# Attention scores by head strips with gate tiles between the levels, and the first MLP product by seven products of blocks

## The chip, the cores and the metric

The kernel runs on one core of one Trainium2 chip. The metric is the device time of one execution in microseconds (us); before the change three runs gave 1222.52, 1223.50 and 1223.92, median 1223.5. Engines: PE is TensorE (matrix products into PSUM; PEld its weight loads), DVE is VectorE, ACT is ScalarE, POOL is GpSimd, and SP is SyncE, which here only issues DMAs.

## The reference

One layer of a hybrid backbone for 512 sample tokens and 128 prompt tokens (640 columns in the kernel, `NT`; half of them is `HN` = 320), width 1024, all in float32:

```
h  = rmsnorm(x) * (1 + sc1) + sh1                    # modulated by c or c_ctx (ada_w, 1024 x 6144)
u  = h @ w_in                                        # 1024 x 6432
y  = pooling, Fourier, RWKV-7 (two directions, scan over chunks), GLA (two directions)
GLA: att[t,s] = sum_d q[t,d] k[s,d] decay[t,s,d], 4 heads of 32; o = att @ v + state term
merged = sum_i sigmoid(u_gate[i]) * (y[i] @ w_branch[i])   # 4 branches, 4 x 1024 gate columns of w_in
x  = x + g1 * (merged @ w_out)
h2 = rmsnorm(x) * (1 + sc2) + sh2
x  = x + g2 * (relu(h2 @ mlp_w1)**2 @ mlp_w2)        # 1024 x 4096, 4096 x 1024
y  = rmsnorm(x) * final_g
```

## The kernel before, in words

**Products in two parts.** A large product is made of three: both operands are split into a rounded part (fp32r, `..h`) and a remainder (`..l`), and h*h, h*l and l*h are added in PSUM. A weight tile goes through `load` (L249): `fetch` (L238) issues one DMA on SP into one of three buffers "wr" (128 x 512 floats, 256 KB), and `split` (L244) makes the rounded part on ACT (L246) and the remainder on DVE (L247). `terms` (L363) issues the three products on both halves of the columns, so a tile of 8 blocks of rows is 48 products of 320 columns: this is a column tile of `w_in`, and a gate tile. A branch tile has two blocks, 12 products.

**Order.** The code is traced in program order, and a list scheduler lays down each engine's queue at build time: of what is ready in its model, the earliest traced first. `with hi()` lifts what it traces above that order, `high_priority(offset=...)` shifts it by a number (a negative one lets it fill what others leave), and `tc.issue_after(ins)` lets the instructions traced in it that run on the engine of `ins` stand behind `ins` there. A pool with `bufs=n` gives a tag n buffers; the next tile waits until the oldest is released. At run time each queue is worked off in its order.

**Stages.** (1) Norm, modulation, input projection (`columns` writes 15 tiles to DRAM, `uscr`), pooling and Fourier. (2) RWKV in two pairs of heads (L686): a scan of 8 steps (L915) of small products; `new_x` (L848) copies values into the next state tile on POOL (L854). Gate and branch tiles of branches 0 and 1 and gate tiles of branch 2 (L1218 to L1224), traced later, fill PE meanwhile; gates of branch 2 go to DRAM (`gscr`) and come back for `merged(2, ...)` (L1226). (3) GLA: for each of seven levels (L1056; half sizes p = 64 down to 1) `eq` and `ek` are made on DVE and ACT, `eq` is copied head by head into a tile `eqm` that is zero outside a head's 32 partitions (L1080), and for each of the five token tiles one product of 512 columns (4 heads x 128) gives the scores (L1084), of which a masked copy (L1091 on DVE, for the two first levels L1089 on ACT) goes to `att`. Then states and outputs to L1176. (4) Last branch and output projection (L1252): per `dt` the gate tiles of branch 3, two ahead (L1254), branch 3, the sum of all branches split in two parts (L1263, L1264), two tiles of `w_out`, and products for four token tiles (L1247); `ada_rest` (L319) makes part of the modulation on DVE (L309) from 256 KB tiles. (5) Second half of that projection, residual, norm, transposes into `nh` and `nl` (L1326).

**MLP.** Four groups of 8 column tiles. `hidden` (L1356) makes one column tile for one half of the tokens: 24 products (L1361), then ReLU on ACT, square on DVE, and the split into `fh` and `fl` (L1365 to L1368). Then the second product of the group (L1407) for two halves of the output columns, 5 token tiles each, in five banks; `residual` (L1392) multiplies each sum with g2 and adds it to `xf` in two DVE passes. The last half of the last group has its weights at hand (L1416) and is followed tile by tile by the last norm and the output.

Of the kernel before, what the change touches and what calls it, by code (L numbers as in the profile page):

```python
# [14 lines left out]
ALU = mybir.AluOpType  # L15
# [121 lines left out]
def backbone(ctx, tc, a, y_prompt, y_sample, out_rwkv, out_gla):  # L137
# [100 lines left out]
    def fetch(src):  # L238
        n, c = src.shape[1:]
        raw = wpool.tile([P, 512], F32, name="wr", tag="wr", bufs=3)[:, : n * c].rearrange("p (k c) -> p k c", c=c)  # L240
        nc.sync.dma_start(out=raw, in_=src)
        return raw

# [118 lines left out]

    def terms(pt, wh, wl, k, c0, mh, ml, start, stop):  # L363

        lh, ll = wh[:, k, c0 : c0 + P], wl[:, k, c0 : c0 + P]
        for n, (w, m) in enumerate(((lh, mh), (lh, ml), (ll, mh))):
            for b in range(2):
                PE.matmul(pt[:, b, :HN], lhsT=w, rhs=m[:, b * HN : b * HN + HN],  # L368
                          start=start and n == 0, stop=stop and n == 2)
# [252 lines left out]

    def split_into(y, j, src):
# [62 lines left out]
    for hp in range(2):  # L686
# [161 lines left out]
        def new_x(step):  # L848

            x = upool.tile([P, 4, 2, 2, 64], F32, name="xc", tag="xc", bufs=3)  # L850
            for smp in (True, False)[: 2 if step < 2 else 1]:
                ch = slice(0, 2) if smp else slice(2, 4)
                for O_, par in ((HR[0], 1), (HR[1], 0)):
                    (S.copy if step == 0 else G.tensor_copy)(x[O_, ch, par], pick(VT, step, smp)[O_].unsqueeze(2).broadcast_to([64, 2, 2, 64]))  # L854
# [130 lines left out]

    pb.close()
# [23 lines left out]
    eqm = [gpool.tile([P, 4, NT], F32, name=f"eqm{j}") for j in range(2)]  # L1010
# [45 lines left out]
    for n in range(7):  # L1056
# [18 lines left out]
        else:  # L1075
            ek = kg
        em = eqm[n % 2]
        for h in range(4):
            hr = slice(32 * h, 32 * h + 32)
            S.copy(em[hr, h, :], eq[hr, :])  # L1080
        for i in range(5):
            ts_ = slice(i * P, i * P + P)
            pt = pxt()
            PE.matmul(pt, lhsT=ek[:, ts_], rhs=em[:, :, ts_], start=True, stop=True)  # L1084
            pt = pt.rearrange("p (h t) -> p h t", h=4)
            if p >= 32:
                for s0 in range(0, P, p):
                    rows, cols = slice(s0, s0 + p), slice(s0 ^ p, (s0 ^ p) + p)
                    S.copy(att[rows, :, i, cols], pt[rows, :, cols])  # L1089
            else:  # L1090
                V.copy_predicated(att[:, :, i, :], lm[:, n, :].unsqueeze(1).broadcast_to([P, 4, P]), pt)  # L1091
# [86 lines left out]

    def load_y(n, pool=mgpool):
        y = new_y(pool)  # L1180
        for j in range(2):
            t = zpool.tile([P, NT], F32, name="mg", tag="mg", bufs=2)
            nc.sync.dma_start(out=t, in_=yscr[n][j])
            split_into(y, j, t)
        return y

    def gate(i, dt):
        pt = proj(C_GATE + i * D + dt * P)
        g = zpool.tile([P, NT], F32, name="gate", tag="gate", bufs=3)
        with hi():  # L1190
            S.activation(v2(g), pt, AF.Tanh, scale=0.5)
        return g

    def branch(i, dt, y):
        bh_, bl_ = load(a["t_branch"][i, dt], wpool, "b", 1)
        pt = pm.tile([P, 2, 512], F32, name="pt", tag="pm")
        for k in range(2):
            terms(pt, bh_, bl_, k, 0, y[0][:, k, :], y[1][:, k, :], k == 0, k == 1)
        return pt

    gscr = [dpool.tile([P, NT], F32, name=f"gscr{k}") for k in range(KT)]

    def load_sum(n, dt):
        m = zpool.tile([P, NT], F32, name="mg", tag="mg", bufs=2)
        nc.sync.dma_start(out=m, in_=mscr[n][dt])
        return m

    def gated(g, pt):
        V.scalar_tensor_tensor(v2(g), v2(g), 1.0, pt[:, :, :HN], ALU.add, ALU.mult)

    def merged(i, dt, g, pt):
        with hi():
            gated(g, pt)
            if i > 0:
                V.tensor_tensor(g, load_sum(i - 1, dt), g, ALU.add)
            nc.sync.dma_start(out=mscr[i][dt], in_=g)

    for i, y in ((0, y_a), (1, load_y(0))):  # L1218
        for dt in range(KT):
            merged(i, dt, gate(i, dt), branch(i, dt, y))  # L1220
    for dt in range(KT):
        g = gate(2, dt)
        with hi():
            nc.sync.dma_start(out=gscr[dt], in_=g)  # L1224
    y_r = load_y(2, yrpool)
    for dt in range(KT):  # L1226
        g = zpool.tile([P, NT], F32, name="gate", tag="gate", bufs=3)
        nc.sync.dma_start(out=g, in_=gscr[dt])
        merged(2, dt, g, branch(2, dt, y_r))
# [20 lines left out]
    gates = [gate(3, 0), gate(3, 1)]  # L1250
    accs = [po.tile([P, 512], F32, name="po", tag="po") for _ in range(4)]
    for dt in range(KT + 2):  # L1252
        if dt + 2 < KT:
            gates.append(gate(3, dt + 2))  # L1254
# [28 lines left out]
    nh = h2.tile([P, KT, NT], F32R, name="nh")  # L1283
    nl = h2.tile([P, KT, NT], F32R, name="nl")
    pf1 = ctx.enter_context(tc.tile_pool(name="pf1", bufs=3, space=PSUM, reuse_waits="tile"))
    ops = ExitStack()
# [14 lines left out]
    def projected(i, hf, acc, t):  # L1301
        c = i // 4
        if c not in g1b:
            g1b[c] = h2.tile([P, D], F32, name="g1b", tag="g1b")
# [4 lines left out]
        S.activation(t[:, bs], xf[i][:, bs], AF.Square, accum_out=ss[:, 2 * i + hf : 2 * i + hf + 1])  # L1309

# [14 lines left out]

    def transposed(i, t):  # L1326
        c = i // 4
        sl_ = slice(i * P, i * P + P)
        for k4 in range(2):
# [3 lines left out]
            tm = op.tile([P, 4, P], F32, name="tm", tag="tm", bufs=2)  # L1333
            for k in range(4):
                kk = k4 * 4 + k
                S.activation(tm[:, k], pt[:, k * P : k * P + P], AF.Identity, scale=s2[:, kk, c : c + 1], bias=b2[:, kk, c : c + 1])
            ks = slice(k4 * 4, k4 * 4 + 4)
            S.copy(nh[:, ks, sl_], tm)
            V.tensor_tensor(nl[:, ks, sl_], tm, f32(nh[:, ks, sl_]), ALU.subtract)
# [14 lines left out]
    with tc.tile_pool(name="mlp", bufs=1, reuse_waits="tile") as mp, \  # L1354
            tc.tile_pool(name="pf2", bufs=5, space=PSUM, reuse_waits="tile") as pf2:
        def hidden(w, h, l, b):  # L1356
            pt = pbank()
            bs = slice(b * HN, b * HN + HN)
            for k in range(KT):
                for n, (wk, m) in enumerate(((w[0], nh), (w[0], nl), (w[1], nh))):  # L1360
                    PE.matmul(pt[:, :HN], lhsT=wk[:, k, :], rhs=m[:, k, bs], start=k == 0 and n == 0,  # L1361
                              stop=k == KT - 1 and n == 2)
            with hi():
                rl = mp.tile([P, HN], F32, name="rl", tag="rl", bufs=3)
                S.activation(rl, pt[:, :HN], AF.Relu)  # L1365
                V.tensor_tensor(rl, rl, pt[:, :HN], ALU.mult)  # L1366
                S.copy(h[:, bs], rl)
                V.tensor_tensor(l[:, bs], rl, f32(h[:, bs]), ALU.subtract)  # L1368

        g2b = mp.tile([P, 2, D], F32, name="g2b")  # L1370
        gf = mp.tile([P, D], F32, name="gf")
        NG = 4
        for g in range(NG):
            ws, fh, fl = [], [], []
            order = [(f, b) for f in range(8) for b in range(2)]
            if g == 0:
                order[:4] = [(0, 0), (1, 0), (0, 1), (1, 1)]
            for f, b in order:
                if b == 0:
                    ws.append(load(a["t_w1"][g * 8 + f]))  # L1380
                    fh.append(mp.tile([P, NT], F32R, name="fh", tag="fh", bufs=11))
                    fl.append(mp.tile([P, NT], F32R, name="fl", tag="fl", bufs=11))
                elif f == 0 and g == 0:
# [86 lines left out]
```

## Time and profile before

| | |
|---|---|
| median of three runs | 1223.5 us |
| the profiled execution, its own time | 1224.66 us |
| its span, first to last instruction | 1222.9 us |
| mean granted clock of TensorE | 0.988 |
| instructions | 19633 |
| DMA | 147.41 MB, mean 121 GB/s |

The span is read from the start of the first instruction; the stages meet at about 536 (GLA), 614 (its last level), 650 (last branch), 731, 767 (MLP) and 1213 (last product). Busy time of an engine is the union of its instructions; products are pipelined, so the mean time of one (309 ns) is longer than the step from one to the next (147 ns).

### The profile page before, as it was taken

Reading aid. Unit: us, or ns where it says so; the run is one execution under the profiler, and the core shown is the slowest. Engines: PE = TensorE matmul, PEld = TensorE weight load, DVE = VectorE, ACT = ScalarE, POOL = GpSimd, SP = SyncE. Lnnn points to the kernel's source line nnn. Section 1 sums busy time; section 2 is a strip of 40 time slices with the busy share of each in tenths; the row PEclk is TensorE's granted clock in tenths of the full one; section 3 lists DMA queues with packets and bytes.
Section 4 is the critical chain, followed back from the end, with each engine's and each line's share of the span. In section 5 each row is a group of like instructions: output and inputs, shape, how many; then the busy total and the mean of one; then the engine's idle time right before and its main releaser. Section 6 shows DMA issues by size and latency. Waiting matters only on the chain.

```text
span 1222.9 us, 19633 instructions
## 1 busy us (share of the span) xinstructions
PE 1176.4 (96%) x7556; PEld 1017.1 (83%) x7556; DVE 733.5 (60%) x1458; ACT 506.7 (41%) x1028; POOL 62.3 (5%) x98
## 2 busy tenths in 40 slices
PE   7999999899999999997999989999999999999996
PEld 2778998789778898795588978998899899889985
DVE  4797785675588583447987757543443354245456
ACT  4732225742376522378635325532143123213332
POOL 0000000500114200300000000000000000000000
PEclk9999898999999999999999999999999999999999
DMA  9558661334314343056624560322222222222222
GB/s 357 205 173 251 201 224 57 104 93 119 101 36 122 103 148 95 30 170 212 195 93 141 179 208 18 99 75 69 77 79 85 71 79 78 70 87 69 78 87 86
DMA packets 85971, 147.41 MB, mean 121 GB/s; under 512 B 21693, under 2 KB 26206, under 8 KB 85878
## 3 DMA queue, kind: packets, MB, share of 16 engines
q1 hardware_dynamic: 85878, 146.16, 37.8%
q8 instruction: 59, 0.97, 0.3%
q14 instruction: 34, 0.28, 0.1%
HBM read 123.17 MB, written 22.95 MB: 119 GB/s over the span
## 4 chain that ended last, share of the span: by engine, by line
PE 77%; DVE 8%; DMA 7%; ACT 4%; issue 3%; SPq 0%; POOL 0%; DVEq 0%; ACTq 0%; POOLq 0%
PE pt L368 23%; PE pf L1361 18%; PE pf L1407 16%; PE po L1247 3%; PE pf L1427 2%; PE px L1084 2%; DMA araw<-in_t_ada_dram 2%; PE px L499 2%; DVE acc L309 2%; DVE wl L247 1%; PE px L287 1%; DMA wr<-in_t_in_dram 1%; DMA wr<-in_t_out_dram 1%; DMA wr<-in_t_w_dram 1%; PE px L775 1%
## 5 line engine op out<-in xcount | busy, mean ns | idle before, releaser
L246 ACT CAST wh<-wr 128x512 fp32r<-128x512 f32 x222 | 133.4, 618 | 349.5 <-PE pf L1407 139.1
L247 DVE TENSOR_TENSOR wl<-wr,wh 128x512 fp32r<-128x512 f32 x222 | 152.2, 700 | 206.9 <-ACT wh L246 202.4
L368 PE MATMUL pt<-xl,wh 128*128 128x320 f32 x816 | 200.5, 321 | 0.0
L368 PE MATMUL pt<-xh,wh 128*128 128x320 f32 x816 | 199.7, 321 | 0.0
L368 PE MATMUL pt<-xh,wl 128*128 128x320 f32 x816 | 196.1, 318 | 0.0
L1361 PE MATMUL pf<-nh,wl 128*128 128x320 f32 x512 | 158.1, 309 | 0.0
L1361 PE MATMUL pf<-nl,wh 128*128 128x320 f32 x512 | 158.0, 309 | 0.0
L1361 PE MATMUL pf<-nh,wh 128*128 128x320 f32 x512 | 157.9, 309 | 0.0
L368 PEld LDWEIGHTS pt<-xh,wh 128*128 128x128 f32 x816 | 138.9, 191 | 8.8 <-issue 4.1
L368 PEld LDWEIGHTS pt<-xl,wh 128*128 128x128 f32 x816 | 139.5, 191 | 6.8 <-issue 3.0
L368 PEld LDWEIGHTS pt<-xh,wl 128*128 128x128 f32 x816 | 138.9, 191 | 4.9 <-issue 1.7
L1407 PE MATMUL pf<-wl,fh 128*128 128x512 f32 x280 | 109.0, 389 | 0.0
L1407 PE MATMUL pf<-wh,fh 128*128 128x512 f32 x280 | 109.0, 389 | 0.0
L1407 PE MATMUL pf<-wh,fl 128*128 128x512 f32 x280 | 108.9, 389 | 0.0
L1361 PEld LDWEIGHTS pf<-nl,wh 128*128 128x128 f32 x512 | 96.0, 187 | 0.2
L1361 PEld LDWEIGHTS pf<-nh,wh 128*128 128x128 f32 x512 | 96.0, 188 | 0.1
L1361 PEld LDWEIGHTS pf<-nh,wl 128*128 128x128 f32 x512 | 96.0, 187 | 0.0
L309 DVE SCALAR_TENSOR_TENSOR acc<-araw,sc,acc 128x512 f32<-128x512 f32 x112 | 78.4, 746 | 11.9 <-DMA araw<-in_t_ada_dram 11.9
L1407 PEld LDWEIGHTS pf<-wh,fl 128*128 128x128 f32 x280 | 52.6, 188 | 11.0
L1407 PEld LDWEIGHTS pf<-wh,fh 128*128 128x128 f32 x280 | 52.6, 188 | 10.9
L1407 PEld LDWEIGHTS pf<-wl,fh 128*128 128x128 f32 x280 | 52.6, 188 | 10.7
L1366 DVE TENSOR_TENSOR rl<-rl,pf 128x320 f32<-128x320 f32 x64 | 31.0, 484 | 39.0 <-ACT rl L1365 39.0
(540 smaller groups left out, 1754.2 us busy)
## 6 DMA issues: line engine op xcount, KB each, us to landing
wr<-in_t_w_dram SPq DMA_DIRECT2D x128, 256.0 KB, 3.0
wr<-in_t_in_dram SPq DMA_DIRECT2D x102, 256.0 KB, 3.5
araw<-in_t_ada_dram SPq DMA_DIRECT2D x64, 256.0 KB, 3.5
adaw<-in_t_ada_dram SPq DMA_DIRECT2D x16, 512.0 KB, 9.2
mscr<-gate SPq DMA_DIRECT2D x24, 320.0 KB, 4.3
mg<-mscr SPq DMA_DIRECT2D x24, 320.0 KB, 3.8
uscr<-mg SPq DMA_DIRECT2D x15, 320.0 KB, 2.8
wr<-in_t_branch_dram SPq DMA_DIRECT2D x32, 128.0 KB, 2.1
```

The costliest lines, as they stand in the source:

```text
L246: S.copy(wh, raw)
L247: V.tensor_tensor(wl, raw, f32(wh), ALU.subtract)
L287: PE.matmul(pt[0:8, :], lhsT=c[:, 4 * part : 4 * part + 8, k + j], rhs=w[:, j], start=part == 1 and k + j == 0 and n == 0, stop=part == 0 ...
L309: V.scalar_tensor_tensor(acc[j], raw, w, acc[j], ALU.mult, ALU.add)
L368: PE.matmul(pt[:, b, :HN], lhsT=w, rhs=m[:, b * HN : b * HN + HN], start=start and n == 0, stop=stop and n == 2)
L499: PE.matmul(pt[:, :HN], lhsT=lhsT, rhs=rhs[:, b * HN : b * HN + HN], start=True, stop=True)
L1084: PE.matmul(pt, lhsT=ek[:, ts_], rhs=em[:, :, ts_], start=True, stop=True)
L1247: PE.matmul(acc, lhsT=m[k][:, sl_], rhs=W[k, hf][w][:, 0, :], start=k == 0 and n == 0, stop=k == KT - 1 and n == 2)
L1361: PE.matmul(pt[:, :HN], lhsT=wk[:, k, :], rhs=m[:, k, bs], start=k == 0 and n == 0, stop=k == KT - 1 and n == 2)
L1366: V.tensor_tensor(rl, rl, pt[:, :HN], ALU.mult)
L1407: PE.matmul(acc[i], lhsT=m[k][:, ts_], rhs=w[:, kk, :], start=k == 0 and n == 0, stop=k == 7 and n == 2)
L1427: PE.matmul(acc, lhsT=m[k][:, ts_], rhs=ws[k][w][:, 0, :], start=k == 0 and n == 0, stop=k == 7 and n == 2)
```

## The change

**Scores.** Of each level, the four sample token tiles are now computed per head as strips: 32 partitions of `ek` against the same 32 of `eq`, 128 x 128 scores each, 16 products into four PSUM banks, one per head. Only the prompt's token tile still goes through `eqm` (now 128 columns) into a fifth bank; the pool has four. Copies to `att` stay as many.

**Gates.** The tiles of branches 0 and 1 and the gates of branch 2 are traced before GLA at a priority lowered by 200000. The gate tiles of branch 3 are no longer made in the last stage: tile n - 1 stands on PE behind the prompt's product of level n - 1, and the strips of level n stand behind it. They go to DRAM and come back in the last stage; tiles 6 and 7 follow the levels. Weight tiles of branch 2 get three buffers of their own.

**First MLP product.** `mlp_w1` is laid out as 2 x 2 blocks (`kh`: half of the rows; `fh_`: which of the two column tiles of a pair), 16 pairs. Seven products of 12 give both column tiles for both halves of the tokens (Strassen's scheme in Winograd's form). Four products use sums of weight blocks, read from DRAM tiles `wsum`. For the first group these are made by eight DRAM-to-DRAM DMAs on POOL's queue (four copies, four accumulating), one behind a copy of `new_x` per step of the scan; for the others, DVE adds them during the second product of the group before, with loads on SP and stores on POOL's queue. Five block sums of the normalised input are made on DVE and ACT after the last transposes, while the first three pairs take the products that need none; the transposes write a plain tile `nf`, and `nh`, `nl` keep the first 320 tokens only.

**Residual.** `xf` is stored to DRAM (`xres`) and holds the plain MLP sum (ACT copy in the first group, one DVE pass in the next two); g2 and the stored residual are applied in the last group.

```diff
-        "t_w1": blocks(x["mlp_w1"][0], range(0, FF, P), P),
+        "t_w1": np.ascontiguousarray(blocks(x["mlp_w1"][0], range(0, FF, P), P).reshape(16, 2, P, 2, 512).transpose(3, 1, 0, 2, 4)),
...
+        def begin(n, g):
+            src = w1b[(0, 0, 1, 1)[n], (0, 1, 1, 0)[n], 4 * g : 4 * g + 4]
+            return lambda: nc.gpsimd.dma_start(out=rows(wsum[n][g]), in_=rows(src))
+
+        def add(n, g):
+            src = (w1b[0, 1, 4 * g : 4 * g + 4], w1b[1, 1, 4 * g : 4 * g + 4], wsum[0][g], wsum[2][g])[n]
+            return lambda: nc.gpsimd.dma_start(out=rows(wsum[n][g]), in_=rows(src), accum_op=ALU.add, max_dma_last_dim=8192)
...
+            if step > 0:
+                chore(1, last)
...
+    with tc.high_priority(offset=-200000):
+        for i, y in ((0, y_a), (1, load_y(0))):
+            for dt in range(KT):
+                merged(i, dt, gate(i, dt), branch(i, dt, y))
+        for dt in range(KT):
+            gate_out(0, dt)
...
+        banks = [pxt() for _ in range(4)]
+
+        if n > 0:
+            with tc.issue_after(scored.ins):
+                gate_out(1, n - 1)
+        with hi(), tc.issue_after(newest[0].ins) if n > 0 else ExitStack():
+            for i in range(4):
+                ts_ = slice(i * P, i * P + P)
+                for h in (3, 2, 1, 0):
+                    hr = slice(32 * h, 32 * h + 32)
+                    PE.matmul(banks[h][:, ts_], lhsT=ek[hr, ts_], rhs=eq[hr, ts_], start=True, stop=True)
+
         em = eqm[n % 2]
         for h in range(4):
             hr = slice(32 * h, 32 * h + 32)
-            S.copy(em[hr, h, :], eq[hr, :])
-        for i in range(5):
-            ts_ = slice(i * P, i * P + P)
-            pt = pxt()
-            PE.matmul(pt, lhsT=ek[:, ts_], rhs=em[:, :, ts_], start=True, stop=True)
+            S.copy(em[hr, h, :], eq[hr, NS:])
+        bank = pxt()
+        scored = PE.matmul(bank, lhsT=ek[:, NS:], rhs=em.rearrange("p h t -> p (h t)"), start=True, stop=True)
...
-    gates = [gate(3, 0), gate(3, 1)]
+    gates = [gate_back(1, 0), gate_back(1, 1)]
...
+        put("22", a22)
+        V.tensor_tensor(a22, a22, a21, ALU.subtract)
+        put("22-21", a22)
+        V.tensor_tensor(a21, a11, a21, ALU.subtract)
+        V.scalar_tensor_tensor(a11, a22, -1.0, a11, ALU.mult, ALU.subtract)
+        put("21-22-11", a11)
+        put("11-21", a21)
+        V.scalar_tensor_tensor(a12, a11, -1.0, a12, ALU.mult, ALU.subtract)
+        put("22-21+11-12", a12)
...
+        def product(pt, m, src, first):
+
+            with hi():
+                wh, wl = load(src.unsqueeze(1), mp, "st", 4)
+                wh, wl = wh[:, 0], wl[:, 0]
+            mh_, ml_ = A[m]
+            for k in range(4):
+                ks = slice(k * P, k * P + P)
+                for n, (w, x) in enumerate(((wh, mh_), (wh, ml_), (wl, mh_))):
+                    PE.matmul(pt[:, :HN], lhsT=w[:, ks], rhs=x[:, k, :], start=first and k == 0 and n == 0,
+                              stop=k == 3 and n == 2, skip_group_check=True)
...
+        def pair_steps(j):
...
+            product(ba, "11", b11, True)
+            with hi():
+                S.copy(p1, ba)
+            yield
+            product(bb, "21-22-11", wsum[2][g][q], True)
+            with hi():
+                V.tensor_tensor(u2, p1, bb, ALU.add)
+            yield
+            product(ba, "12", b21, False)
...
+            product(bc, "22-21", wsum[0][g][q], True)
+            product(bb, "11-21", wsum[1][g][q], False)
+            with hi():
+                V.tensor_tensor(u3, p1, bb, ALU.add)
+                c = st()
+                V.tensor_tensor(c, u3, bc, ALU.add)
+                S.activation(c, c, AF.Relu, scale=-1.0)
+                S.activation(c, c, AF.Square)
+                parts_of(c, h1, l1, t1)
+            yield
+            product(bb, "22", wsum[3][g][q], False)
...
+            product(bc, "22-21+11-12", b22, False)
...
+            def weight_sums(g, q):
+
+                b11, b12, b21, b22 = (trp.tile([P, 512], F32, name="tr", tag="tr", bufs=4) for _ in range(4))
+                with tc.issue_after(loaded[0].ins):
+                    for t, (kh, fh_) in ((b11, (0, 0)), (b12, (0, 1)), (b22, (1, 1)), (b21, (1, 0))):
+                        nc.sync.dma_start(out=t, in_=w1b[kh, fh_, 4 * g + q])
+                for n, t, s in ((0, b11, b12), (1, b12, b22), (2, b22, b11), (3, b21, b22)):
+                    V.tensor_tensor(t, t, s, ALU.add)
+                    nc.gpsimd.dma_start(out=wsum[n][g][q], in_=t)
```

## Rows read from the trace of the kernel before

**Rows 1.** The page, busy time (us), share of the span and instructions.
```profile
PE 1176.4 (96%) x7556; PEld 1017.1 (83%) x7556; DVE 733.5 (60%) x1458; ACT 506.7 (41%) x1028; POOL 62.3 (5%) x98
```

**Rows 2.** The chain that ended last: start us, us, what.
```profile
605.58 8.85 PE px L1084 x20
...
742.75 0.87 PE pf L1332 x8
...
756.31 10.90 PE po L1247 x48
...
880.40 56.32 PE pf L1361 x384
```

**Rows 3.** Stages: us, busy us and count per engine, PE clock, DMA share, GB/s.
```profile
300.00:352.00 52.00, 51.42 (x621) 39.66 (x621) 28.00 (x71) 22.18 (x54) 5.45 (x12) 1.00 0.21 62
...
552.00:614.00 62.00, 53.73 (x201) 32.44 (x200) 53.84 (x91) 46.26 (x90) 0.00 (x0) 0.97 0.62 194
614.00:650.00 36.00, 33.61 (x229) 29.48 (x228) 30.01 (x54) 15.26 (x25) 0.00 (x0) 1.00 0.32 101
650.00:731.00 81.00, 77.86 (x440) 68.84 (x440) 52.39 (x81) 29.84 (x51) 0.00 (x0) 0.98 0.57 187
...
826.00:880.00 54.00, 54.00 (x239) 44.68 (x238) 19.54 (x32) 9.74 (x18) 0.00 (x0) 1.00 0.25 78
880.00:936.00 56.00, 56.00 (x383) 55.95 (x382) 27.56 (x53) 21.82 (x46) 0.00 (x0) 1.00 0.25 76
...
1158.00:1185.00 27.00, 27.00 (x121) 22.37 (x120) 11.24 (x18) 9.17 (x16) 0.00 (x0) 1.00 0.35 107
```

**Rows 4.** Stages, products of L368 alone: us, PE and PEld busy us and count.
```profile
552.00:614.00 62.00, 23.47 (x121) 17.92 (x119) 0.97 0.62 194
614.00:650.00 36.00, 20.39 (x114) 17.17 (x114) 1.00 0.32 101
650.00:731.00 81.00, 52.87 (x336) 51.01 (x336) 0.98 0.57 187
```

**Rows 5.** ACT in order of time, the casts of w21 and w27.
```profile
1174.24 0.62 ACT L246 CAST w21h<-wr 128x512 fp32r<-128x512 f32 x1 [1.18 <-DMA wr<-in_t_w_dram]
...
1182.64 0.62 ACT L246 CAST w27h<-wr 128x512 fp32r<-128x512 f32 x1 [0.98 <-DMA wr<-in_t_w_dram]
```

**Rows 6.** Groups by line and shape: count | busy us, mean ns | idle before.
```profile
L247 DVE TENSOR_TENSOR wl<-wr,wh 128x512 fp32r<-128x512 f32 x222 | 152.2, 700 | 206.9 <-ACT wh L246 202.4 <-PE pt L368 3.6 <-issue 0.2
L246 ACT CAST wh<-wr 128x512 fp32r<-128x512 f32 x222 | 133.4, 618 | 349.5 <-PE pf L1407 139.1 <-PE pt L368 113.4 <-PE pf L1361 59.7
...
L1368 DVE TENSOR_TENSOR fl<-rl,fh 128x320 fp32r<-128x320 f32 x64 | 31.5, 492 | 14.2 <-ACT fh L1367 14.2
...
L775 PE MATMUL px<-sl,big 64*128 64x128 f32 x160 | 18.2, 290 | 5.9 <-ACT sl L781 3.4 <-DVE big L757 2.1 <-ACT big L758 0.2
L1091 DVE COPY_PREDICATED att<-lm,px 128x512 f32<-128x512 int32 x25 | 17.2, 735 | 0.4
...
L283 DVE TENSOR_TENSOR adal<-adaw,adah 128x1024 fp32r<-128x1024 f32 x8 | 9.7, 1221 | 2.1 <-ACT adah L282 2.1
```

**Rows 7.** ACT in order of time, the last tokens' modulation.
```profile
775.62 1.19 ACT L1336 ACTIVATE tm<-pf,b,s 128x128 f32<-128x128 f32 x3
```

**Rows 8.** The page, GB/s moved in 40 equal slices.
```profile
GB/s 357 205 173 251 201 224 57 104 93 119 101 36 122 103 148 95 30 170 212 195 93 141 179 208 18 99 75 69 77 79 85 71 79 78 70 87 69 78 87 86
```

**Rows 9.** DMA issues: count, KB each, median us to landing.
```profile
wr<-in_t_w_dram SPq DMA_DIRECT2D x128, 256.0 KB, 3.0
...
gate<-gscr SPq DMA_DIRECT2D x8, 320.0 KB, 4.6
```

**Rows 10.** PE in order of time, half-array products in the scan's preparation.
```profile
231.69 1.25 PE L775 MATMUL px<-sl,big 64*128 64x128 f32 x16 [0.48 <-DVE big L757]
232.87 0.56 PE L368 MATMUL pt<-xh,wl 128*128 128x320 f32 x2
233.27 0.45 PE L368 MATMUL pt<-xh,wh 128*128 128x320 f32 x2
```

More of the change, by code (lines that the diff above doesn't have):

```diff
@@ L1009, in backbone @@
     G.memset(att, 0.0)
-    eqm = [gpool.tile([P, 4, NT], F32, name=f"eqm{j}") for j in range(2)]
+    eqm = [gpool.tile([P, 4, P], F32, name=f"eqm{j}") for j in range(2)]
     for j in range(2):
@@ L1176, in backbone @@
         V.scalar_tensor_tensor(y_out[j], og[j], 0.5, y_out[j], ALU.mult, ALU.mult)
[L1179 to L1224, printed above, removed]
+    for dt in (6, 7):
+        gate_out(1, dt)
     y_r = load_y(2, yrpool)
     for dt in range(KT):
-        g = zpool.tile([P, NT], F32, name="gate", tag="gate", bufs=3)
-        nc.sync.dma_start(out=g, in_=gscr[dt])
-        merged(2, dt, g, branch(2, dt, y_r))
+        merged(2, dt, gate_back(0, dt), branch(2, dt, y_r))
     y_g = new_y()
@@ L1253, in backbone @@
         if dt + 2 < KT:
-            gates.append(gate(3, dt + 2))
+            gates.append(gate_back(1, dt + 2))
         if dt < KT:
@@ L1324, in project, with block_sums, put @@
             projected(i, hf, acc, t)
+    def block_sums(pool):
+        a11, a12, a21, a22 = nf[:, 0:4, t0], nf[:, 4:8, t0], nf[:, 0:4, t1], nf[:, 4:8, t1]
+        r = {}
+        def put(name, s):
+            h, l = (pool.tile([P, 4, HN], F32R, name=f"{n}{name}") for n in ("sh", "sl"))
+            S.copy(h, s)
+            V.tensor_tensor(l, s, f32(h), ALU.subtract)
+            r[name] = (h, l)
+        put("22", a22)
[7 more added lines that the diff above has]
+        put("22-21+11-12", a12)
+        return r
+    t0, t1 = slice(0, HN), slice(HN, NT)
     def transposed(i, t):
@@ L1372, in backbone @@
         NG = 4
         for g in range(NG):
-            ws, fh, fl = [], [], []
-            order = [(f, b) for f in range(8) for b in range(2)]
+            fh, fl = [], []
+            before_ = None
             if g == 0:
[L1377 to L1383, printed above, removed]
-                    with hi():
-                        transposed(4, before)
-                    ops.close()
-                hidden(ws[f], fh[f], fl[f], b)
@@ L1388, in backbone @@
-            if g == 0:
+                now = first_pairs()
+                next(now)
+                with hi():
+                    transposed(4, before)
+                    ops.close()
+                    A.update(block_sums(spool.enter_context(tc.tile_pool(name="spool", bufs=1, reuse_waits="tile"))))
+                nfs.close()
+                trs = ExitStack()
+                trp = trs.enter_context(tc.tile_pool(name="trpool", bufs=1, side="right", reuse_waits="tile"))
+                for _ in now:
+                    pass
@@ new lines, in backbone @@
+            for j in range(0 if g else 3, 4):
+                now = pair_steps(4 * g + j)
+                next(now)
+                if before_:
+                    next(before_)
+                next(now)
+                if before_:
+                    next(before_)
+                next(now)
+                before_ = now
+            next(before_)
+            next(before_)
+            if g == NG - 1:
+                spool.close()
+                trs.close()
+                h2pool.close()
+                w2pool = ExitStack()
+                w2p = w2pool.enter_context(tc.tile_pool(name="w2pool", bufs=1, side="right", reuse_waits="tile"))
+                g2b = w2p.tile([P, 2, D], F32, name="g2b")
+                gf = w2p.tile([P, D], F32, name="gf")
@@ L1411, in backbone @@
                         residual(i, hf, acc[i])
-        h2pool.close()
-        with tc.tile_pool(name="w2pool", bufs=1, side="right", reuse_waits="tile") as w2p:
+        with w2pool:
             ws = [load(a["t_w2"][(NG - 1) * 4 + k // 2, 1, :, k % 2 : k % 2 + 1], w2p, f"w2{k}", 1) for k in range(8)]
```

207 lines of the change are left out of this document (177 added, 30 removed).

## The prediction

> **What bounds the kernel now.** I read the page's busy line first: PE holds 96% of the span, DVE 60%, ACT 41% [rows 1]. The chain in order of time says where PE alone counts: from 774 us on, the MLP is unbroken runs of PE pieces, such as 384 first products in 56.32 us [rows 2], and the stage table has PE busy for 56.00 of 56.00 us there and DVE for 27.56 [rows 3]. A product less is time won there, if DVE, ACT and the DMA keep up. Earlier, from 552 to 731 us, PE is idle 8.3, 2.4 and 3.1 us in three stages, while DVE is busy 53.84 of 62, 30.01 of 36 and 52.39 of 81 us [rows 3]: PE first, DVE close behind. In the last of the three, 240 of the 336 products of L368 are five gate tiles of 48 (the other 96 are branch products) [rows 4]; in the first, the attention scores take 31 us (below).
>
> **First MLP product.** A pair of column tiles takes 2 x 2 halves x 8 k x 3 terms = 96 products of 320 columns; seven products of blocks take 7 x 4 x 3 = 84. Over 16 pairs 192 go, at 56.32 / 384 = 0.147 us [rows 2]: -28.2 us, all on the path.
>
> What must hide beside the rest: (a) Weights. A pair fetches 7 tiles instead of 4, one per 12 products, 1.76 us. The three "wr" buffers gave a fetch each 1.40 us when nothing else held them: w21h to w27h, six fetches in 8.40 us [rows 5]. A buffer's round is so 4.2 us and may grow to 5.3. (b) DVE per pair: 7 splits of 0.700 and 11 sums, squares and remainders of 0.492 [rows 6], 4.9 + 5.4 = 10.3 of 12.3 us; ACT has 7 casts of 0.618 [rows 6] and 9 short passes that I set at DVE's 0.49, 8.7. Both fit, DVE narrowly. For places where a product waits until DVE has read its bank (the last pair of a group has no neighbour between its steps) I take +2; bounds 0 and, if waits stretch a round to 5.7 us, 112 x (1.90 - 1.76) = +16. (c) The block sums of the normalised input: five splits and four differences of 1280 columns. DVE takes 1221 ns for 1024 columns and 700 for 512 [rows 6], so about 1.48 for 1280: 9 x 1.48 = 13.3 us. PE has 6 products before it needs the first, 10.6 us, and 8 transposed blocks at 0.87 [rows 2], from 767.2 to 778.7. The last tokens leave ACT at 776.8 [rows 7]; a cast (set at 1.3) and a remainder (1.48) put the first block at 779.6. The next two follow 4.3 and 4 us apart, with splits of weights on the same DVE, against 5.3 us of products each. I take +4; bounds 0 and +10, most of the DVE work uncovered. (d) The residual's last step saves DVE work that PE hides already: 0. The old residual comes back in the last group's stage, 10 passes over 1024 columns (1.22 each, 12.2 us) beside 11.24 us of DVE in 27 [rows 3]: 0, bound +3.
> MLP: -28.2 + 2 + 4 = -22; bounds -28 and -2.
>
> **Weight sums.** For group 0, eight DRAM-to-DRAM transfers of 1 MB stand on POOL's queue, each behind a copy of the scan, and the scan's next copies behind them. POOL is busy 5.45 of 52 us there and the DMA moves 62 GB/s [rows 3]; 8 MB more in that time makes 216, under the 357 of the first slice [rows 8]. No row shows a DMA from POOL. If each held POOL for the 3.0 us in which a 256 KB load lands [rows 9], seven in one scan make 21, partly hidden, as PE fills with gate tiles: bounds 0 and +12; I take +2, near nothing, as POOL idles nine tenths. For groups 1 to 3 four loads on SP stand behind a fetch of the second stage and the next fetch behind them; their buffers must be back from POOL's stores, begun two steps (60 of 239 products in 54 us, 13.6 us) before [rows 3]. DVE adds 16 x 0.70 = 11 us to 19.54 of 54 [rows 3]. 0, bound +4.
>
> **Scores and gates, 552 to 731 us.** Scores now: 35 products of 512 columns, 70 rows (these fp32 products show two rows each), at 8.85 / 20 = 0.44 us [rows 2], 31.0 us. After: 7 products for the prompt, 14 rows, 6.2 us; and 112 strips of 32 partitions x 128 columns, 224 rows. A full product of 128 columns takes 0.87 / 8 = 0.109 a row [rows 2]: one after another 24.4, four beside each other 6.1 us. The nearest row is that of the half arrays, two groups: 16 rows from 231.69 to 232.87, 0.074 each [rows 10], and 18.2 / 160 = 0.114 over all, gaps in the pipeline included [rows 6]. I take 0.09 for two and half of that for four: 10.0 us. Coming back to full products cost 0.40 us where two products take 0.29 [rows 10]; I set in and out at 0.3, 2.1 in seven. Sum 18.3, a gain of 12.7; bounds 0 and 18.7.
>
> The Trainium skill (TensorEngine Tiling (Array Packing), Performance Considerations) warns that array tiling speeds up TensorE and not the emptying of PSUM, which may then be the bound. The trace bears out the size: a level's five banks take 5 x 0.735 = 3.7 us of DVE [rows 6] against 2.6 of PE. By that rule alone the strips would give nothing and the sum would come out 12.7 us higher; here a gate tile, 7 us of PE, lies over the emptying.
>
> Now by stages. Levels: scores 18.3, six gate tiles of 48 x 0.147 = 7.04 (42.2), 96 branch products (14.1), 1.1 of transposes: 75.7. The prompt's product needs a fifth bank of four, so it waits until the first is emptied (0.735 and signals), and the 48 gate products stand behind it on PE; branch products can fill in. +4 for these holes: 80, against 62 now. DVE, at 53.84 plus eight more splits (5.6), bounds no longer. Tail of the mixer, 614 to 650: a chain of DVE and ACT; its 114 gate products become 96: 36 as now. Last stage: 81 less five gate tiles (35.2) leaves 45.8 for PE; DVE, 52.39 less ten splits (6.9), 45.5; the DMA moves 81 x 187 = 15.1 MB [rows 3], less 2.6 of gate weights, plus 2.6 of gates read back, 42 us at 357 GB/s. Three floors within 4 us of each other: I take 49. In all 165 against 179: -14. Bounds: strips side by side, no holes and a last stage of 46 give 152 (-27); serial strips and a last stage in which sixteen W_out tiles pass one free buffer at 4.2 us (67) give 195 (+16).
>
> **Sum.** The profiled run took 1224.66 us, 1.76 more than its span. -22 + 2 - 14 = -34 gives 1190.7; the runs' median lies 1.16 below the profiled run, so 1189.5, said as 1190.
>
> **Rivals.**
> A, slower: the three "wr" buffers set the pace of the products. With the 4.6 us in which gates landed [rows 9] in place of 3.0, and 1 us in DVE's queue, a round is 6.8 us, 2.27 a fetch, 112 x 0.51 = 57 us: 1247. It decides from a round of 6.2 us on (2.07 a fetch, 34 us lost). For it: DVE at 84%, 1.1 us of slack. Against: four tiles of look-ahead and a DMA share of 0.25 now [rows 3]. 6%.
> B: the gates leave the last stage, but DVE, the DMA and single buffers keep it at 62: region -1, 1203. For it: three floors together; against: each is under 46. 19%.
> C: the strips run one after another: +12.7, 1203. For it: half arrays gained a third at best [rows 10]. 9%.
> D: POOL's transfers delay the scan, and filler runs out before the levels: +10, 1200. 6%.
> E: no holes, no waits, each stage at its floor: 1190 - 13 - 5 = 1172. 12%.
> The forecast itself, 1180 to 1199: 48%.
>
> **How the numbers follow.** What a measurement can tell from no change is 0.2%, 2.4 us. The range leaves out E's lower half and most of A: 1174 to 1216. Faster: all but A and a joint failure of B, C and D, 0.90; same 0.03; slower 0.07.
>
> **What would show it.** First products of a group in 49.3 us instead of 56.3, PE without gaps, a fetch each 1.76 us (A: PE waits for the split of weights). Near 780 us, PE waits of 2 to 6 us for block sums. Strips at 0.04 to 0.05 us a row (C: 0.1). Gate products between the levels; from the last level's end to the MLP's first product 36 + 49 + 36 = 121 us (B: 134; now 153). The scan ends no later than now (D: later). The forecast is wrong if a group's first products take over 52 us, or if PE's idle time before the MLP grows by more than 15.

## The result, and the profile after

The changed kernel takes 1278.5 us (median of four runs, 1271.7 to 1284.1) where the kernel before, run beside it, takes 1223.0 (1219.3 to 1223.9): a ratio of 1.046, 95% interval 1.039 to 1.053. The forecast was 1190. The profiled execution took 1283.74 us with a span of 1282.0, so 59.1 us more than the span of before.

The page's busy line of after, as [rows 1]: TensorE works 15.7 us less than before, in a span that is 59 us longer. The work went down as planned, and the idle time grew by 75 us.

```profile
PE 1160.7 (91%) x7532; PEld 1002.7 (78%) x7532; DVE 816.5 (64%) x1577; ACT 535.2 (42%) x1103; POOL 89.0 (7%) x154
```

Five marks on TensorE's own instructions, the same in every kernel, show where. They are in us from the span's start: the first score product, the last one, the last product of the mixer's attention, the first product of the MLP, and the end.

| | score, first | score, last | mixer, last | MLP, first | end |
|---|---|---|---|---|---|
| before | 560.2 | 614.4 | 640.2 | 767.8 | 1222.9 |
| after | 568.4 | 650.6 | 676.0 | 841.1 | 1282.0 |
| difference of each stretch | +8.2 | +28.0 | -0.4 | +37.5 | -14.2 |

The levels were meant to grow, since six gate tiles were put in there. That they come out near the forecast's 80 us is luck: the 14.1 us of branch 2 products that it counted there are missing, and longer waits and a lower clock stand in their place. And the stretch behind the mixer, which was to give it all back and more, grew by 37.5 us as well.

Stages of after (length, busy us and count of each engine, TensorE's clock, DMA share, GB/s), to be held against [rows 3]:

```profile
566.00:650.00 84.00, 68.33 (x537) 60.56 (x538) 39.46 (x68) 37.83 (x95) 0.00 (x0) 0.86 0.19 60
650.00:683.00 33.00, 32.59 (x222) 28.43 (x220) 17.15 (x35) 11.81 (x19) 0.00 (x0) 1.00 0.19 64
683.00:720.00 37.00, 21.00 (x97) 20.04 (x98) 20.45 (x31) 5.91 (x13) 0.00 (x0) 0.72 0.84 264
720.00:801.00 81.00, 44.70 (x188) 31.76 (x187) 51.98 (x79) 16.20 (x28) 0.00 (x0) 0.81 0.60 196
```

The last stage of before had TensorE at work for 77.86 of 81 us. Now there are two stages: one of 37 us with 97 products, 84 of them branch 2's (14 us of work at the 0.147 us a product of before), and one of 81 us with 44.70 us of work. The levels move 60 GB/s where they moved 194: branch 2's loads, sums and stores are no longer in them. The chain of waits of after (start, us, what) says what the two late stages wait for:

```profile
690.75 3.37 DMA wr<-in_t_branch_dram
695.41 4.20 DMA gate<-gscr
700.60 3.55 PE pt L372 x12
706.98 5.53 DMA gate<-gscr
713.56 3.55 PE pt L372 x12
718.59 5.10 DMA wr<-in_t_out_dram
...
735.61 3.48 DMA araw<-in_t_ada_dram
739.20 1.43 DVE acc L311 x2
740.64 3.86 DMA araw<-in_t_ada_dram
744.59 1.43 DVE acc L311 x2
...
797.12 1.22 DMA grow<-grow
798.41 3.55 DMA g1b<-grow
```

Where before ran TensorE work end to end, the chain now steps from one landing to the next: a branch tile of 12 products (3.55 us, where 12 x 0.147 is 1.8), then a wait for a gate tile; two ada weight tiles, 1.43 us of VectorE, then a wait for two more. In the kernel before, the ada product of the last stage began at 609.9 us, and half of its steps ran before 650, beside the mixer's tail; now it begins at 737.4, behind branch 2.

In the MLP, the chain of after shows a group's first products as 45.71 + 3.64 = 49.35 us, as forecast (49.3), and, ahead of that, the first group waiting for the block sums:

```profile
853.93 1.76 ACT nf L1421 x5
857.69 1.17 ACT sh L1395
858.88 1.50 DVE sl L1396
...
957.41 45.71 PE pf L1456 x312
1004.05 3.64 PE pf L1456 x24
```

### The profile page after: what moved, and what is told of

Read it like the earlier page. It is cut to its first block, busy times and chain, and to the rows that moved or that the text cites. A ratio compares the mean times of both kernels' runs of the same rounds, so it can differ in the third digit from the quotient of the medians.

```text
span 1282.0 us, 20248 instructions
## 1 busy us (share of the span) xinstructions
PE 1160.7 (91%) x7532; PEld 1002.7 (78%) x7532; DVE 816.5 (64%) x1577; ACT 535.2 (42%) x1103; POOL 89.0 (7%) x154
## 4 chain that ended last, share of the span: by engine, by line
PE 69%; DVE 10%; DMA 10%; ACT 6%; issue 4%; SPq 0%; POOL 0%; DVEq 0%; ACTq 0%; POOLq 0%
PE pt L372 26%; PE pf L1456 13%; PE pf L1657 13%; PE po L1304 3%; DMA araw<-in_t_ada_dram 3%; DVE acc L311 2%; PE pf L1676 2%; PE px L503 2%; DVE wl L249 1%; PE px L289 1%; DMA wr<-in_t_branch_dram 1%; DMA wr<-in_t_out_dram 1%; ACT wh L248 1%; PE px L806 1%; PE pxc L977 1%
## 5 line engine op out<-in xcount | busy, mean ns | idle before, releaser
L372 PE MATMUL pt<-xh,wh 128*128 128x320 f32 x816 | 204.3, 327 | 0.0
L248 ACT CAST wh<-wr 128x512 fp32r<-128x512 f32 x158 | 94.5, 618 | 240.5 <-PE pt L372 132.5
L249 DVE TENSOR_TENSOR wl<-wr,wh 128x512 fp32r<-128x512 f32 x158 | 108.0, 701 | 91.6 <-ACT wh L248 88.1
L249 DVE TENSOR_TENSOR stl<-wr,sth 128x512 fp32r<-128x512 f32 x112 | 77.0, 691 | 49.0 <-ACT sth L248 47.5
L248 ACT CAST sth<-wr 128x512 fp32r<-128x512 f32 x112 | 69.0, 618 | 86.1 <-PE pf L1456 51.3
L1644 POOL DMA_DIRECT2D wsum<-tr x48 | 26.0, 541 | 601.7 <-DVE tr L1643 598.4
L1643 DVE TENSOR_TENSOR tr<-tr 128x512 f32<-128x512 f32 x48 | 33.1, 690 | 32.1 <-DMA tr<-in_t_w_dram 31.2
L1463 ACT CAST fh<-sums 128x320 fp32r<-128x320 f32 x64 | 29.2, 459 | 28.7 <-DVE sums L1575 16.4
L1456 PE MATMUL pf<-nh,sth 128*128 128x320 f32 x128 | 40.0, 312 | 1.0 <-ACT sums L1491 0.9
L1456 PE MATMUL pf<-nh,stl 128*128 128x320 f32 x128 | 39.7, 311 | 0.4 <-DVE stl L249 0.4
```

The source lines that it names most:

```text
L248: S.copy(wh, raw)
L249: V.tensor_tensor(wl, raw, f32(wh), ALU.subtract)
L372: newest[0] = PE.matmul(pt[:, b, :HN], lhsT=w, rhs=m[:, b * HN : b * HN + HN], start=start and n == 0, stop=stop and n == 2)
L1456: PE.matmul(pt[:, :HN], lhsT=w[:, ks], rhs=x[:, k, :], start=first and k == 0 and n == 0, stop=k == 3 and n == 2, skip_group_check=True)
L1463: S.copy(h[:, bs], x)
L1643: V.tensor_tensor(t, t, s, ALU.add)
```

## The experiments

Line numbers in the rows are each kernel's own. Theories and rivals carry the letters of the expectations here. "Levels" is the stretch between the first two marks, "late stretch" that from the mixer's last product to the MLP's first.

**First set: which part loses.** A gate tile, or a product, is called bound here where `tc.issue_after` ties its place on TensorE to the scores. mlp_only is the kernel before with the MLP hunks of the change; scores_gates is before with the other hunks. strips_free is the changed kernel with this edit:

```diff
-        if n > 0:
-            with tc.issue_after(scored.ins):
-                gate_out(1, n - 1)
-        with hi(), tc.issue_after(newest[0].ins) if n > 0 else ExitStack():
+        with hi():
...
-    gates = [gate_back(1, 0), gate_back(1, 1)]
+    gates = [gate(3, 0), gate(3, 1)]
```

(and `gate(3, dt + 2)` in the last stage's loop). branch2_bound is the changed kernel with branch 2 bound as well:

```diff
             with tc.issue_after(scored.ins):
+                merged(2, n - 1, gate_back(0, n - 1), branch(2, n - 1, y_r))
+                if n > 4:
+                    merged(2, n + 1, gate_back(0, n + 1), branch(2, n + 1, y_r))
                 gate_out(1, n - 1)
```

with `y_r` loaded ahead of the levels and the later loop over `merged(2, ...)` gone. What was expected:

> The MLP part alone (seven products, weight sums, the POOL transfers beside the RWKV scan); scores, gates and the last mixer stage as in the kernel before. Theory A (the moved gates displaced the branch 2 products, and the lost time is all in the last stage): the MLP gives back about the 13 us that it gave in the changed kernel, the slower scan takes some 6 to 8 of them, so 1216 to 1219 us. Rival B (the slower scan and the paced sums are what also wrecked the stages behind): the stage before the projection grows here too, and the time is 1250 or more.

> The scores by strips and the moved gates alone, with the MLP of before and without the POOL transfers. Theory A: the whole loss stands here, last stage about 118 us as in the changed kernel, and the scan at its old pace, so 1280 to 1290 us. Rival B (scan and sums): the last stage is near its old 81 us and the time is 1210 to 1235.

> The changed kernel with the gates of branch 3 back in the last stage, where the kernel before has them; strips, seven products and sums kept. Theory A: the branch 2 products run beside the levels again and the last stage is near 81 us, the levels shrink by what the strips save (12.7 us by the forecast, less if the level chain on VectorE and ScalarE sets the pace), MLP minus 13, scan plus 8: 1203 to 1215 us. Rival C (the strips themselves lengthen the levels, since emptying four banks per level is slower than the five small ones): levels of 60 us or more, and 1222 to 1235. Rival B: 1240 or more.

> The changed kernel with the branch 2 products bound between the levels too, one ahead of each moved gate (two in the last two levels). Theory A: branch 2's 96 matmuls (13.6 us) go into the levels, which grow by 5 to 14 us; the buffers of branch 2 come free before the levels end, the ada product starts beside the mixer's tail, and the last stage falls from 118 to between 49 and 75 us: total 1222 to 1250. Rival D (the last stage is held by transfers: the gates' read-back and the output weights beside the ada weights, whatever the order): last stage 95 or more, total 1265 to 1285.

Measured, beside 1222.0 us for the kernel before (18 runs, 1216 to 1228); every ratio, here and below, is to the runs of the kernel before that stood beside that kernel's own:

| | median us | ratio (95%) | levels | late stretch | MLP |
|---|---|---|---|---|---|
| before | 1222.0 | | 54.2 | 127.6 | 455.1 |
| after | 1278.5 | 1.046 (1.039 to 1.053) | 82.2 | 165.1 | 440.9 |
| mlp_only | 1208.8 | 0.990 (0.987 to 0.993) | 53.6 | 124.4 | 440.8 |
| scores_gates | 1294.9 | 1.061 (1.056 to 1.066) | 83.0 | 169.2 | 454.6 |
| strips_free | 1214.2 | 0.993 (0.990 to 0.996) | 59.9 | 121.7 | 440.6 |
| branch2_bound | 1238.3 | 1.014 (1.009 to 1.018) | 97.6 | 106.2 | 440.4 |

Theory A holds: the MLP itself is 14 us shorter wherever the new one stands, and the other part alone loses 73. Taking the bound gates back undoes the loss; binding branch 2 into the levels as well gives 59 us of late stretch back for 15 of levels. Rivals B and D fall: the late stretch is as before with the new MLP, and it shrinks by the order alone. Three figures were missed: mlp_only came out 7 us better than forecast, scores_gates 5 us worse, and in strips_free the levels didn't shrink by what the strips save; they are 6 us longer than mlp_only's, the 60 us of rival C, though its total is in theory A's range.

Stages of branch2_bound, in the same columns (levels, tail, last stage):

```profile
565.00:663.00 98.00, 81.39 (x632) 72.94 (x631) 54.83 (x91) 38.63 (x98) 0.00 (x0) 0.90 0.46 146
663.00:697.00 34.00, 31.55 (x205) 26.86 (x203) 24.43 (x45) 11.53 (x19) 0.00 (x0) 0.95 0.35 110
697.00:761.00 64.00, 47.83 (x206) 35.45 (x207) 50.06 (x77) 21.76 (x39) 0.00 (x0) 0.90 0.67 222
```

Even so placed, the move doesn't pay: from the first score product to the first product of the MLP TensorE is busy 195.6 of 230.8 us, where in the kernel before it is 195.5 of 207.6. The gates were never in the way of a stage with room elsewhere; they filled the last stage to 96% (77.86 of 81 us), and the levels, at 53.73 of 62, had no room for 42 us more.

**Second set: order or buffers, gates or strips, and who paces the levels.** after_own_buffers gives the branch 2 step buffers of its own:

```diff
+        if n == 0:
+            g = yrpool.tile([P, NT], F32, name="gback", tag="gback", bufs=2)
...
+        if apart:
+            raw = yrpool.tile([P, 512], F32, name="wrb", tag="wrb", bufs=2)
```

gates_alone puts the five masked products per level back in place of strips, gates still bound (its branch 2 weights also lose the three buffers of their own that the change gave them). strips_ekpool and mlp_ekpool change one line of strips_free and mlp_only:

```diff
-            V.tensor_tensor(ek, ek, kg, ALU.mult)
+            G.tensor_tensor(ek, ek, kg, ALU.mult)
```

> The changed kernel, in which the branch 2 step has buffers of its own for the gates that it reads back and for the raw weights that it fetches, so that it can't queue behind the bound gates for a buffer; the order of the work is unchanged. Theory A (the order: the bound gates hold TensorE until the levels are over, and branch 2 stands behind them in its program): its loads are issued earlier, its products don't move by more than a few us, total 1262 to 1285. Rival E (the rings of buffers, which rotate in the order of the program's text, hold branch 2 back): its products move into the levels, the last stage falls by 30 us or more, total below 1250.

> The changed kernel with the scores of before (five masked products per level, no strips), the gates still bound between the levels. Against strips_free (strips without the bound gates) and mlp_only (neither). Theory A (the bound gates alone make the loss; strips are worth next to nothing since VectorE and the level's own chain set the levels): 1262 to 1285, levels of 80 us or more, the last stage as in the changed kernel. Rival F (it is strips and bound gates together: the fifth product waits for a bank that VectorE must empty, and the gates queue behind it): levels about 70, and 10 us or more below the changed kernel also for that reason, 1250 to 1262.

> strips_free with one of VectorE's two 128x640 multiplies of each level (the key side) on GpSimd, which does nothing there. Theory G (VectorE sets the pace of the levels: 48.8 us busy of 60, so a cheaper TensorE buys nothing): 6 multiplies of 0.82 us leave VectorE, the levels fall from 60 to about 55 and the time by 3 to 6 us, to 1208 to 1211. Rival H (the levels wait for banks and for the chain exponent, multiply, strips, empty; a slower multiply on GpSimd lengthens it): levels 60 to 66, 1214 to 1222.

> mlp_only (scores and gates as before) with the same multiply on GpSimd. Theory G: levels from 53.6 to about 49 us, but what TensorE doesn't do there it does in the last stage, which is full (114 of 118 us busy before), so 1204 to 1209. Rival H: levels longer, 1209 to 1216.

Measured, beside 1221.1 us for the kernel before (7 runs, 1218.9 to 1225.7):

| | median us | ratio (95%) | levels | late stretch |
|---|---|---|---|---|
| after_own_buffers | 1281.9 (one run) | | 81.3 | 161.3 |
| gates_alone | 1278.1 | 1.044 (1.040 to 1.049) | 78.0 | 168.4 |
| strips_ekpool | 1207.0 | 0.987 (0.983 to 0.990) | 49.9 | 125.0 |
| mlp_ekpool | 1204.1 | 0.986 (0.982 to 0.989) | 52.2 | 125.4 |

The buffers of gates and raw weights aren't the cause, so rival E falls for these. The products of branch 2 in after (count: shortest, median and longest ns, first and last start):

```profile
L372 PE MATMUL pt<-yh,brh x32: 303/348/607, 680.7 to 715.6; 128*128 128x320 f32 x32
```

In after_own_buffers they start at 682.6 us, no earlier:

```profile
L376 PE MATMUL pt<-yh,brh x32: 302/310/604, 682.6 to 714.4; 128*128 128x320 f32 x32
```

Yet there the first weights of branch 2 and the last half of its input were split, and so ready for TensorE, more than 120 us before. VectorE's remainders of both (start, us):

```profile
535.90 0.81 DVE L253 TENSOR_TENSOR brl<-wrb,brh 128x256 fp32r<-128x256 f32 x2 [3.37 <-ACT brh L252]
555.90 0.83 DVE L660 TENSOR_TENSOR yl<-mg,yh 128x640 fp32r<-128x640 f32 x1 [0.31 <-ACT yh L659]
```

So neither the loads nor these two rings of buffers held the products. The two PSUM buffers `pt`, which gate and branch tiles share, go round in the order of the text too, where the gates of branch 3 come first; no run separates them from the place in TensorE's queue.

gates_alone equals the changed kernel: the bound gates alone make the loss. Its levels are full, 76.65 us of TensorE in 79:

```profile
568.00:647.00 79.00, 76.65 (x361) 57.14 (x362) 37.77 (x61) 45.83 (x87) 0.00 (x0) 0.96 0.20 65
```

Against that, after's levels have 8 us less TensorE work and are 4 us longer, for the reason that rival F gives (the fifth product and the gate behind it wait), but without its effect on the total. The groups of after's levels (count, busy us, mean ns, idle before and who ended it):

```profile
L1179 PE MATMUL px<-gt 32*128 32x128 f32 x224 | 10.1, 306 | 0.1
L1186 PE MATMUL px<-eqm,gt 128*128 128x512 f32 x13 | 9.6, 824 | 15.5 <-DVE att L1195 9.1 <-ACT att L1193 6.4
```

The strips take 10.1 us, 0.045 a row, just the estimate of the forecast: that is the pace of four beside each other. What they save is paid back at the fifth product, which waits 15.5 us in all for a bank to be emptied, with the gate behind it. Without bound gates VectorE is the busiest engine of the levels, with strips or without. In the columns of the stages, the levels of mlp_only come first:

```profile
557.00:611.00 54.00, 46.73 (x165) 27.10 (x164) 47.83 (x81) 39.57 (x78) 0.00 (x0) 1.00 0.61 184
```

Then those of strips_free:

```profile
560.00:620.00 60.00, 48.34 (x347) 37.31 (x346) 48.82 (x82) 30.47 (x84) 0.00 (x0) 0.85 0.58 182
```

And those of strips_ekpool:

```profile
561.00:611.00 50.00, 43.60 (x309) 32.52 (x310) 41.52 (x66) 29.19 (x82) 9.47 (x7) 0.83 0.49 154
```

VectorE is busy 81 to 89% of each. With one multiply a level off VectorE, strips_ekpool's levels are 10 us shorter and its time 7, as theory G has it, but by twice its 5 us: seven other passes of VectorE (two gates and two sums of branch 2, three steps of the ada product) fell behind the last score as well. In mlp_ekpool the levels gained only 1.4 us where theory G said 4.6; its gain over mlp_only, 4.7 us of medians with intervals that overlap, is not settled.

**Third set: where the rest of the MLP's gain is.** All on mlp_ekpool. no_block_sums (its products take the first block of activations in place of the five sums) and no_weight_sums (groups 1 to 3 take plain weight blocks, nothing is loaded, added or stored for sums) leave out those parts of the computation:

```diff
+        for name in ("22", "22-21", "21-22-11", "11-21", "22-21+11-12"):
+            r[name] = (nh[:, 0:4], nl[:, 0:4])
```

and, for the second,

```diff
-                    if g < NG - 1 and k2 % 2 == 1:
-                        weight_sums(g + 1, hf * 2 + k2 // 2)
```

ek_wsum_pool makes the weight sums' additions on GpSimd, and ek_wsum_merge the addition of the merged sum of branch 2 too:

```diff
-                    V.tensor_tensor(t, t, s, ALU.add)
+                    G.tensor_tensor(t, t, s, ALU.add)
...
-                V.tensor_tensor(g, load_sum(i - 1, dt), g, ALU.add)
+                (G if i == 2 else V).tensor_tensor(g, load_sum(i - 1, dt), g, ALU.add)
```

> mlp_ekpool with the five sums of blocks of the activations left out (their products take the first block instead, so the output differs): the same products, banks, weights and transfers. In mlp_only the first products take 208.6 us where 1344 at the old 0.147 us would be 197.6; 11 us more, most of it in the first 50 us of the MLP. Theory I (the block sums stand on the path there: the copy of the last tile's block, 3.4 us, then subtractions): the first products fall by 5 to 8 us, total 1196 to 1200. Rival J (the waits for banks that ScalarE and VectorE empty make the excess, whatever the operands): less than 2 us, 1202 to 1207.

> mlp_ekpool without the sums of weight blocks for groups 1 to 3 (their products take plain blocks, so the output differs): 48 additions on VectorE, 48 loads more on SyncE's queue and 48 stores on GpSimd's are gone. Theory K (these steps cost the 3.8 us by which the second products are slower than before, 222.2 against 218.4 us, by VectorE's time and by transfers): second products 218 to 219, total 1199 to 1202. Rival L (they are hidden, and the second products are slower for another reason, such as the new accumulation in the output tiles): within 1 us of 222, total 1203 to 1206.

> mlp_ekpool with the 48 additions of the weight sums on GpSimd in place of VectorE. By theory K in its VectorE form, 1 to 4 us less, 1200 to 1203; by rival L the same, 1203 to 1206; should GpSimd be so late with the sums that the first products wait for them, 1208 or more.

> ek_wsum_pool with the addition of the merged sums of branch 2 (8 of 0.82 us, beside the levels) on GpSimd too. Theory G (VectorE sets the levels): levels from about 52 to 48 us, and 2 to 4 us of it reach the end, 1198 to 1202; if the levels are now set by TensorE and the level's chain, 1202 to 1206.

The two sums in the table add the steps from each product's start to the next one's, over the MLP.

| | median us | ratio (95%) | first products, us | second products, us |
|---|---|---|---|---|
| before | 1221.2 | | 226.2 | 218.4 |
| mlp_only | 1208.8 | 0.990 (0.987 to 0.993) | 208.6 | 222.2 |
| mlp_ekpool | 1204.1 | 0.986 (0.982 to 0.989) | 208.0 | 221.3 |
| no_block_sums | 1197.7 | 0.980 (0.977 to 0.983) | 201.1 | 223.1 |
| no_weight_sums | 1207.2 | 0.988 (0.986 to 0.991) | 209.0 | 219.6 |
| ek_wsum_pool | 1202.8 | 0.984 (0.981 to 0.987) | 208.7 | 220.0 |
| ek_wsum_merge | 1211.8 | 0.993 (0.990 to 0.995) | 209.5 | 220.6 |

Theory I holds: the block sums cost the first products 6.9 us, and the time fell by 6.4. Without the weight sums the second products take 1.7 us less, and with their additions on GpSimd 1.3. That is one trace each, and the second products of the nine kernels that differ elsewhere spread from 221.2 to 223.1 us, so this is no more than a hint. no_weight_sums' total, 1207.2, is outside the ranges of both K and L: theory K isn't shown. ek_wsum_merge was expected to gain and lost 9 us against ek_wsum_pool. Its levels did fall, from 51.9 to 47.4 us, as theory G has it; but its tail took 30.6 us for 25.0 and its late stretch 128.9 for 124.7. From the levels' start to the tail's end VectorE is busy 68.3 us in the one (79 us) and 68.2 in the other (77 us), though eight additions had left it; the last section shows how. The best kernels are ek_wsum_pool, mlp_ekpool, strips_ekpool and mlp_only, 1.0 to 1.6% faster than before. All have the new MLP and no bound gates, and the intervals of the first three overlap.

## Why the prediction was wrong

Rivals carry the letters of the prediction from here on.

**The step that failed** is in the sum of the levels: "96 branch products (14.1)" and "branch products can fill in". The forecast left branch 2 where the profile of before has it, in the levels. There it was filler, taken because TensorE had nothing of higher rank. The change puts a gate tile, tied to the scores, into each of these holes; branch 2 comes later in the text, got its turn only at 680 us, when the last gate tile of branch 3 was through, and everything that follows from it (its gate tiles read back, the release of its input, the ada product that takes that memory) moved behind the mixer. In after_own_buffers its operands were ready at 556 us and its products still came at 682.6. The forecast counted 45.8 us of TensorE, 45.5 of VectorE and 42 of DMA for the last stage and took 49, as if they would overlap; with branch 2 gone from the levels they stood largely one after another for 118 us. branch2_bound restores the assumed order, and its late stretch is 59 us shorter. Of the two signs of being wrong that the forecast named, one came: TensorE's idle time before the MLP grew by 67.5 us.

**The holes in the levels**: taken at 4 us, measured at 15.5. The rule of the Trainium skill that the forecast weighed (TensorEngine Tiling (Array Packing), Performance Considerations: packing speeds up TensorE but not the emptying of PSUM) was set aside with the remark that a gate tile lies over the emptying. The trace bears out the rule: the gate stood behind the product that waited, so nothing lay over the wait. The gain of 12.7 us for the scores came to none, with bound gates (after equals gates_alone) and without (strips_free is not faster than mlp_only). The size of the strips themselves was right (10.1 us for 10.0), and rival C wrong.

**The last stage at 49**: with branch 2 in the levels it is 64 us (697 to 761), close to rival B's 62. No engine is busy for more than 50.06 of them: three loads within 4 us of each other didn't overlap as well as assumed.

**The MLP**, mechanism right, terms undersized: -14.3 us (455.1 to 440.8) for -22. Fewer products: 192 x 0.147, as said. Block sums +6.9 for +4; what is left over 1344 x 0.147 = 197.6 without them is +3.5, all of it in the first group, where 1.5 us are waits for ScalarE to empty a bank (+2 was taken) and the rest stays open; second products +3.8 for 0, of which the weight sums may be 1.3 to 1.7 and the rest stays open. Rival A is wrong: groups 1 to 3 kept their 49.3 us.

**The weight sums of group 0**: with POOL's transfers the scan takes 0 to 4.4 us longer, and 8.8 in after, for +2. From the copy of the first pair's state (`fo`) to that of the second's, the two kernels without them take 166.1 us; of the twelve with them, mlp_only and branch2_bound take 166.1 and 166.2, no_block_sums 167.3, eight 169.7 to 170.5, and after 174.9. The traces tie the longer times to one load: in those nine, VectorE waits 2.3 to 3.4 us for `ut` between 320 and 326 us and a product of the scan waits behind it; in the other five it waits 0.2 us or less. What after has beyond 170 isn't explained. Its wait (in total, times, longest), and the one behind the scan:

```profile
DVE ut L703 <- DMA ut<-uscr: 3.4, 1, 3.4
PE px L1141 <- DMA gt<-uscr: 10.0, 1, 10.0
```

The changed kernel's late start of the levels (+8.2) is a scan that ends 5.1 us later (533.4 for 528.3), and 3.1 us behind it, where TensorE waits 10.0 us for a load of `gt` and has no filler. That looks like rival D but has another cause: all five kernels with bound gates have this wait, of 9.7 to 11.0 us, scores_gates without any transfer on POOL too, and in the others it is 2.2 us at most.

In all, the sum went: start +8.2, levels +28.0, tail -0.4, late stretch +37.5, MLP -14.2, together the 59.1 us.

## What to carry to other kernels

When filler is moved forward to a place with holes, ask what filled these holes until then, and what hangs on it: independent work brought forward pushes dependent work back, where nothing is left to run beside its loads. Add up the bound engine's work over all stages that the move touches; where it is at 92% before (165 of 179 us), moving it can gain no more than the rest, and every added wait takes from that. A product made cheaper is worth its time only if what empties its banks isn't the pace already.

## What the hardware showed

GpSimd's help costs VectorE time. VectorE's instructions of mlp_ekpool in order of time (start, us):

```profile
567.11 0.83 DVE L1098 TENSOR_TENSOR gt<-gt 128x640 f32<-128x640 f32 x1 [1.11 <-ACT gt L1097]
567.86 1.83 DVE L1095 TENSOR_TENSOR gt<-gt 128x320 f32<-128x320 f32 x1
569.60 0.48 DVE L1096 TENSOR_TENSOR gt<-gt 128x320 f32<-128x320 f32 x1
```

GpSimd's in the same stretch:

```profile
567.78 1.55 POOL L1105 TENSOR_TENSOR gt<-gt 128x640 f32<-128x640 f32 x1 [3.61 <-ACT gt L1104]
```

The subtraction of L1095, which takes 0.48 us elsewhere, took 1.83 and ended 0.36 us behind GpSimd's multiply, as if it had begun when that was over. So VectorE was relieved of 0.82 us and lost 1.35. Of the five multiplies in mlp_ekpool's levels two cost VectorE so much (1.35 and 1.26 us) and a third 0.3, where five times 0.82 was saved; that leaves 1.2 us, and the levels are 1.4 shorter. One multiply took 4.39 us for 1.55 beside a row of VectorE's subtractions, so it was GpSimd that lost there; VectorE's masked copies out of PSUM, beside other multiplies, kept their 0.72 to 0.75 us. The Trainium skill (SBUF — State Buffer, Terms) has it that the two share a pair of SBUF ports, held for a whole instruction, and that the loser blocks; these rows agree.

The 32-partition strips run at 0.045 us a row four abreast (10.1 us for 224), against 0.074 for the half arrays of [rows 10]. And TensorE's granted clock was low in the stages where it waited most: 0.72 in the 37 us in which it worked 21.00, 0.81 in the 81 us behind, in which it worked 44.70. It was 0.85 in the strips' levels without bound gates (48.34 of 60 us), against 1.00 in mlp_only's (46.73 of 54). Those stages so ran part of their time at 1.2 GHz, the lower of its two levels.
